# All 128 rows for the small products of a hybrid encoder block, and three norm factors spread by transpositions

## The chip, the cores and the metric

The kernel runs on one core of one Trainium2 chip. The metric is the device time of one execution in microseconds (us); the time given for a kernel is the median of its runs. The chip's engines work side by side, each on its own queue: TensorE (PE; its weight loads are shown apart, as PEld), VectorE (DVE), ScalarE (ACT), GpSimd (POOL), and SyncE (SP), which issues most of the DMA transfers.

## The reference

One layer of a bidirectional encoder on 512 tokens of 1024 channels, with 16 learned meta tokens put in front (528 positions), all in float32:

```
u      = rms_norm(h)
proj   = u @ w_in                                   # split into the parts below
z      = centred_shift(p_rwkv)                      # r, k, v, wd, ad, gd
w_log  = -softplus(-(w0 + tanh(wd) @ w2)) - 0.5     # per direction, rank 64
decay  = exp(-exp(w_log))
a      = sigmoid(a0 + ad @ a2)                      # per direction, rank 64
g      = sigmoid(gd) @ g2                           # rank 160
kk     = (k * k_k) / norm of each head              # the key norm
S_t    = S_{t-1} * decay + (S_{t-1} @ -kk) (kk*a)^T + v k^T ;  y_t = S_t r   # two directions
y_a    = (group_norm(y) + bonus) * g
y_b    = grouped-query attention: q, k rms-normed per head, axial rotary
h      = h + (sigmoid(gA)*(y_a @ wba) + sigmoid(gB)*(y_b @ wbb)) @ w_out
h      = h + square(relu(rms_norm(h) @ w_ff1)) @ w_ff2
out    = rms_norm(h)[:, 16:]
```

The products `tanh(wd) @ w2`, `ad @ a2` and `sigmoid(gd) @ g2` are the low-rank stage. There are 8 heads of 64 channels in the scan, and 8 query heads over 2 key heads in the attention.

## The kernel before, in words

**Precision.** A float32 product is made from products of a rounded type (`F32R`): each operand is split into a high part (a rounded copy, made by ScalarE) and a low part (the difference, made by VectorE or GpSimd), and three of the four part products are summed in PSUM (`mm3`, lines 130 to 134). Weights come in blocks of 128x1024, are split by `wblock` (lines 120 to 128: a DMA, ScalarE for `whi`, VectorE for `wlo`) and have two buffers each. A product whose operands stay plain float32 takes two TensorE instructions, each with its own weight load.

**The first norm.** The input projections of the low-rank part run on x without the norm (`project_steps`, lines 191 and 192). The norm's factor of each token stands in a column per 128 tokens. It is copied over 128 columns (`rx`) and multiplied with the identity matrix, which spreads it along the tokens: line 269 for the four blocks of tokens, line 272 for the meta tokens. `RT` holds the result; `scaled` multiplies by it (lines 275 to 284).

**The low-rank stage.** `stacked` (lines 329 to 337) keeps for each direction d one tile with 128 rows: the high part of the compressed activations in one half, the low part in the other. `constants` (lines 305 to 327) prepares the matrices. For `w2` and `a2` it makes `hh[d]`, the high part copied into both halves (line 316, ScalarE), and `lo`, whose two halves are the low parts of the two directions (line 317, GpSimd). So a product over 128 rows with `hh[d]` gives high times high plus low times high, and a product over the 64 rows of one half with `lo` adds high times low.

- Decay, lines 498 to 516: for each direction and block of 128 tokens, line 506 (128 rows) and line 507 (64 rows) into one PSUM bank, then `w0` is added (line 509, VectorE), the sigmoid (line 510, ScalarE) goes into a tile with the tag `sg` (three buffers), and its split into `sgh` and `sgl` follows (lines 513 and 514). Direction 0 has a fifth block, the 16 meta tokens; its `sg` tile is not split but used as it is.
- Heads, lines 517 to 541: for each direction and each of four pairs of heads, a product with a triangle matrix sums the decays (line 532). For direction 0 the meta tokens have products of their own, in plain float32: line 525 (16 rows) and line 526 (64 rows). Lines 537 (128 rows) and 538 (64 rows) give the rate `a`. Results go to DRAM, from where the scan's preparation reads them.
- Gate, lines 542 to 549: `mm3` on the first 128 ranks, and line 546 on the other 32, whose high and low parts are stacked in 96 rows (`gs`, `sst`).

The PSUM tag `rw` has two banks, which all these products share. Projections of the scan's r, k and v (lines 191 and 192) and the queries (lines 132 to 134) are interleaved with them.

**The scan.** `prepare`, `invert` and `chain` run as generators, with the gate projections fed in between. In `key_norm` (lines 577 to 607) the factors of the keys' norms are spread as in the first norm: line 603 for the tokens, line 598 for the 16 meta tokens, from a tile `rxm` of 16 rows. Most products of the scan use 64 rows or 64 columns.

**The attention.** `attend` (lines 1036 to 1086) runs per head and per half of the queries. The product of the probabilities with the values is line 1076 and line 1077 for four blocks of 128 keys, and line 1078 for the 16 meta keys: `vm` and `pms` have 48 rows, with the high parts in rows 0 to 15, the low parts in rows 32 to 47 and zeros between.

**The feed-forward part.** Its norm factor is spread at line 1223 in the same way as at line 269, and used after the first products of that part.

**Order.** The instructions are traced in program order; a planner then orders each engine's queue by priority with modelled times, gives out the buffers of each tag as they come free, and inserts the waits. `issue_after` keeps some products behind a given one. Each engine's queue is then fixed.

Of the kernel before, what the change touches and what calls it, by code (L numbers as in the profile page):

```python
# [7 lines left out]
F32R = mybir.dt.float32r  # L8
AF = mybir.ActivationFunctionType
ALU = mybir.AluOpType  # L10
# [4 lines left out]
P = 128  # L15
DM = 1024
NM = 16
SEQ = 512
L = NM + SEQ
# [30 lines left out]
def block_kernel(tc, A, out, dbg=None):  # L50
    nc = tc.nc
    v, s, g, pe, sy = nc.vector, nc.scalar, nc.gpsimd, nc.tensor, nc.sync
# [32 lines left out]
    with root:  # L85
# [18 lines left out]

        der = T(cp, [P, 36])
        DC_C0, DC_KKH, DC_KAH, DC_KAB, DC_A0H, DC_RKH = 0, 16, 20, 24, 28, 0
        tmpc = T(cp, [P, 16])
        rkh = T(cp, [P, 4])
        def dcol(c):
            return der[:, c:c + 1]  # L110
# [40 lines left out]
        with ph1:  # L151
# [74 lines left out]
            with ExitStack() as es:  # L226
# [14 lines left out]
                w13 = wblock(A["wrk"][13])  # L241
                sy.dma_start(cst, A["cst"])
                ps12 = whole(project_steps(first, raw))
                g.tensor_tensor(tmpc, par[:, PC_MU0:PC_MU0 + 16], par[:, PC_MU1:PC_MU1 + 16], op=ALU.add)
                g.tensor_scalar(der[:, 0:16], tmpc, -1.0, 1.0, op0=ALU.mult, op1=ALU.add)
                g.tensor_scalar(der[:, 16:20], par[:, PC_KK:PC_KK + 4], 0.5, None, op0=ALU.mult)
# [19 lines left out]
                whole(project_steps(A["wrk"][14], raw, ps14))  # L266
                ps = T(chp, [P, 512], tag="xu", bufs=1)
                for i in range(4):
                    pe.matmul(ps[:, i * P:(i + 1) * P], rx[:, i], ident, start=True, stop=True)
                s.copy(RT[:, NM:L], ps)  # L270
                ps = T(chp, [P, 512], tag="yp", bufs=1)
                pe.matmul(ps[:, 0:NM], rx[:, 4], ident[:, 0:NM], start=True, stop=True)
                s.copy(RT[:, 0:NM], ps[:, 0:NM])

                def scaled(ps):
# [29 lines left out]
                def constants():  # L305

                    c = {}
                    trr = T(wpy, [P, 2, P], F32R)
                    g.tensor_copy(trr, tri)
                    c["tri"] = trr  # L310
                    for n, t in (("w2", w2), ("a2", a2)):
                        hh = [T(wpy, [P, 512], F32R) for _ in range(2)]
                        lo = T(wpy, [P, 512], F32R)
                        for d in range(2):
                            for o in (d, 1 - d):
                                s.copy(hh[d][HF[o]], t[HF[d]])
                            g.tensor_tensor(lo[HF[d]], t[HF[d]], hh[d][HF[d]], op=ALU.subtract)
                        c[n] = hh, lo
                    gh, gl = T(wpy, [P, 512], F32R), T(wpy, [P, 512], F32R)
                    s.copy(gh, gw0)  # L320
                    g.tensor_tensor(gl, gw0, gh, op=ALU.subtract)
                    gs = T(wpy, [96, 512], F32R)
                    for x in (0, 2):
                        s.copy(gs[32 * x:32 * x + 32], gw1)
                    v.tensor_tensor(gs[32:64], gw1, gs[0:32], op=ALU.subtract)
                    c["gw"] = gh, gl, gs
                    return c

# [156 lines left out]
                sh, sl = T(wpz, [P, SEQ], F32R), T(wpz, [P, SEQ], F32R)  # L485
                s.copy(sh, sgd0)
                v.tensor_tensor(sl, sgd0, sh, op=ALU.subtract)
                sst = T(wpz, [96, SEQ], F32R)
                for x in range(2):
                    s.copy(sst[32 * x:32 * x + 32], sgd1)  # L490
                v.tensor_tensor(sst[64:96], sgd1, sst[0:32], op=ALU.subtract)
                keys_values(tk_, qkg, identr)
                xes.close()
                wpy = pool(es, "wdy")
# [3 lines left out]
                with tc.issue_after(started):  # L498
                    sgs = {}
                    for d in range(2):  # L500
                        for i in range(4 if d else 5):
                            n = P if i < 4 else NM
                            c = 64 + i * P if i < 4 else 48
                            ps = bank()
                            hh, lo = con["w2"]
                            pe.matmul(ps[0:n, :], wds[d][:, c - 48:c - 48 + n], hh[d], start=True, stop=False)
                            pe.matmul(ps[0:n, :], wds[d][HF[d], c - 48:c - 48 + n], lo[HF[d]], start=False, stop=True)
                            sg = T(wpy, [P, 512], tag="sg", bufs=3)
                            v.tensor_tensor(sg[0:n, :], ps[0:n, :], w0b[0:n, d, :], op=ALU.add)
                            s.activation(sg[0:n], sg[0:n], AF.Sigmoid)  # L510
                            if i < 4:
                                sgh, sgl = T(wpy, [P, 512], F32R, tag="sgh", bufs=8), T(wpy, [P, 512], F32R, tag="sgl", bufs=8)
                                s.copy(sgh, sg)
                                g.tensor_tensor(sgl, sg, sgh, op=ALU.subtract)
                                sg = sgh, sgl
                            sgs[d, i] = sg
                    for d in range(2):
                        for hp in range(NHP):
                            hc = slice(hp * P, (hp + 1) * P)
                            ab = dcol(DC_A0H + d * 4 + hp)  # L520
                            x0 = 0 if d == 0 else NM
                            lo_ = T(wpy, [P, 2, L], tag="lo", bufs=3)
                            if d == 0:
                                pm = bank()
                                pe.matmul(pm[:, 0:NM], sgs[0, 4][0:NM, hc], tri[0:NM, 0, 0:NM], start=True, stop=True)
                                pe.matmul(pm[:, 16:32], a2[0:64, hc], adz[0:64, 48:64], start=True, stop=True)
                                v.tensor_copy(lo_[:, 0, 0:NM], pm[:, 0:NM])
                                s.activation(lo_[:, 1, 0:NM], pm[:, 16:32], AF.Tanh, scale=0.5, bias=ab)
                            ps = bank()
                            for i in range(4):  # L530
                                for x in range(2):
                                    pe.matmul(ps[:, i * P:(i + 1) * P], sgs[d, i][x][:, hc], con["tri"][:, d, :], start=x == 0, stop=x == 1)
                            v.tensor_copy(lo_[:, 0, NM:L], ps)
                            sy.dma_start(cs_d[hp, d][:, x0:L], lo_[:, 0, x0:L])
                            ps = bank()
                            hh, lo = con["a2"]
                            pe.matmul(ps, hh[d][:, hc], ads[d][:, NM:L], start=True, stop=False)
                            pe.matmul(ps, lo[HF[d], hc], ads[d][HF[d], NM:L], start=False, stop=True)
                            s.activation(lo_[:, 1, NM:L], ps, AF.Tanh, scale=0.5, bias=ab)
                            sy.dma_start(th_d[hp, d][:, x0:L], lo_[:, 1, x0:L])  # L540
                    for hp in range(NHP):
                        hc = slice(hp * P, (hp + 1) * P)
                        ps = bank()
                        gh, gl, gs = con["gw"]
                        mm3(ps, gh[:, hc], gl[:, hc], sh, sl, True, False)
                        pe.matmul(ps, gs[:, hc], sst, start=False, stop=True)
                        gg = T(wpy, [P, SEQ], tag="gg", bufs=2)
                        v.tensor_copy(gg, ps)
                        sy.dma_start(g_d[hp], gg)
# [2 lines left out]

            gtp = pool(ph1a, "gt1", side="right")
            rp = pool(ph1, "rw")
            def load_rkv(hp):
                zs = []
                for x in range(3):
# [19 lines left out]
            def key_norm(hp, zk):  # L577
# [11 lines left out]
                power_mhalf(rn[0:NM, 8:10], rn[0:NM, 8:10])  # L589
                yield  # L590
                rx = G()
                rxm = T(rp, [NM, P], tag="rxm", bufs=1)
                v.tensor_copy(rx[:, 0:512].rearrange("p (a b) -> p a b", b=64), rn[:, 0:8].unsqueeze(2).broadcast_to([P, 8, 64]))
                v.tensor_copy(rxm.rearrange("p (a b) -> p a b", b=64), rn[0:NM, 8:10].unsqueeze(2).broadcast_to([NM, 2, 64]))
                kkh = G("k")
                g.memset(kkh[:, 0:48], 0.0)
                ps = bank()
                pe.matmul(ps[:, 0:NM], rxm, ident[0:NM, 0:NM], start=True, stop=True)
                v.scalar_tensor_tensor(kkh[:, 48:64], zk[:, 48:64], dcol(DC_KKH + hp), ps[:, 0:NM],
                                       op0=ALU.mult, op1=ALU.mult)  # L600
                ps = bank()
# [417 lines left out]
            kll = T(ap_, [P, 2, L], F32R)  # L1019
            vv = T(ap_, [P, 4, 2, P], F32R)  # L1020

            vm = T(ap_, [48, 2, P], F32R)
            pms = [T(ap_, [48, 256], F32R) for _ in range(2)]
            for part, t in ((0, khh), (1, kll)):
                sy.dma_start(t.bitcast(F32), kt_d[part])
            for i in range(4):
                sy.dma_start(vv[:, i].bitcast(F32), vv_d[i])
            lpp = pool(aes, "aloop", side="right")
            zz = T(lpp, [P, 256], tag="yo", bufs=2)[0:48]
            g.memset(zz, 0.0)  # L1030
            for pm in (vm.rearrange("p a b -> p (a b)"), *pms):
                v.tensor_copy(pm, zz)
# [100 lines left out]
        with ExitStack() as es:  # L1133
# [86 lines left out]
            v.tensor_copy(rx, ss[:, 12:16].unsqueeze(2).broadcast_to([P, 4, P]))  # L1220
            ps = fbank("t")
            for i in range(4):
                pe.matmul(ps[:, i * P:(i + 1) * P], rx[:, i, :], ident, start=True, stop=True)
            s.copy(RS, ps)
        dump("h1", h1)

# [150 lines left out]
```

## Time and profile before

| | |
|---|---|
| median of 3 runs | 1050.72 us (1048.79 to 1052.95) |
| the profiled execution | 1051.4 us, of it 1049.6 in the profile's span |
| mean granted TensorE clock in it | 0.968 |
| instructions | 17962 |

The span is what the profile covers; the rest of the execution's time lies around it. The engine lines of a page give busy time, share of the span and number of instructions. A row of a timeline gives start and length in us, engine, line, operation, tiles, rows*columns of the array, the size of what is streamed, and the count; in brackets stands the idle time before it. TensorE's lengths overlap, so the step from one start to the next is what a product costs while nothing else is waited for. A group row gives busy time and mean ns of one, then the idle time before and what ended it. Line numbers are those of the kernel before.

### The profile page before, as it was taken

What the parts mean: (1) busy time and instruction counts of PE and PEld (TensorE: products, weight loads), DVE (VectorE), ACT (ScalarE), POOL (GpSimd) and SP (SyncE); (2) the same over time, 40 slices, a digit from 0 to 9 for tenths busy, and PEclk for the clock granted to TensorE, in tenths of its full rate; (3) what the DMA queues carried; (4) which work ended last, traced back from release to release, by engine and by line L of the source; (5) the groups of instructions that cost most, each with busy time, mean ns of one, the idle gap of its engine ahead of it and who ended that gap; (6) DMA issues with size and microseconds to landing.
All of it is one profiled execution on the core that took longest, in us unless ns stands there. A gap on an engine that the chain in (4) does not pass through costs nothing.

```text
span 1049.6 us, 17962 instructions
## 1 busy us (share of the span) xinstructions
PE 994.9 (95%) x7208; PEld 816.1 (78%) x7208; DVE 592.2 (56%) x1084; ACT 434.4 (41%) x802; POOL 185.9 (18%) x373
## 2 busy tenths in 40 slices
PE   7799989989999899989989999999999999999996
PEld 7778978877767676767777788888888888888885
DVE  4967647756663737396977566455555552123123
ACT  6676434424322524275788533343332232113112
POOL 1266411411411132112311123000000000001001
PEclk9999999999989899886999999999999999999999
DMA  9233662232222211510010284222233332322322
GB/s 348 70 113 86 197 239 71 72 117 100 80 93 92 82 62 62 174 42 11 12 32 21 82 269 132 83 86 95 98 101 101 101 109 92 101 92 89 101 96 85
DMA packets 45508, 107.25 MB, mean 102 GB/s; under 512 B 5264, under 2 KB 12736, under 8 KB 45424
## 3 DMA queue, kind: packets, MB, share of 16 engines
q1 hardware_dynamic: 44848, 105.05, 30.7%
q8 instruction: 57, 0.93, 0.4%
q10 hardware_dynamic: 576, 1.05, 0.3%
q14 instruction: 27, 0.22, 0.1%
HBM read 87.54 MB, written 18.54 MB: 101 GB/s over the span
## 4 chain that ended last, share of the span: by engine, by line
PE 81%; DVE 10%; ACT 4%; issue 2%; DMA 2%; POOL 0%; SPq 0%; ACTq 0%; DVEq 0%; POOLq 0%
PE f L134 8%; PE f L133 8%; PE f L132 8%; PE t L132 6%; PE t L133 6%; PE t L134 6%; PE mm L132 5%; PE mm L133 4%; PE mm L134 4%; PE mm L191 4%; PE mm L192 3%; PE rw L705 2%; PE rw L813 2%; PE yp L869 1%; PE xu L847 1%
## 5 line engine op out<-in xcount | busy, mean ns | idle before, releaser
L126 ACT CAST whi<-wraw 128x1024 fp32r<-128x1024 f32 x118 | 123.7, 1050 | 321.9 <-PE f L134 76.8
L127 DVE TENSOR_TENSOR wlo<-wraw,whi 128x1024 fp32r<-128x1024 f32 x118 | 148.6, 1260 | 183.8 <-ACT whi L126 183.4
L191 PE MATMUL mm<-t,whi 128*128 128x264 f32 x240 | 70.0, 309 | 7.6 <-ACT t L239 7.5
L132 PE MATMUL f<-t,whi 128*128 128x512 f32 x184 | 72.0, 392 | 0.0
L133 PE MATMUL f<-t,whi 128*128 128x512 f32 x184 | 71.7, 390 | 0.0
L134 PE MATMUL f<-t,wlo 128*128 128x512 f32 x184 | 70.9, 390 | 0.0
L192 PE MATMUL mm<-t,whi 128*128 128x264 f32 x240 | 67.7, 299 | 0.0
L133 PE MATMUL t<-wlo,t 128*128 128x512 f32 x160 | 63.4, 396 | 0.0
L133 PE MATMUL f<-wlo,t 128*128 128x512 f32 x160 | 63.3, 396 | 0.0
L134 PE MATMUL f<-whi,t 128*128 128x512 f32 x160 | 63.3, 396 | 0.0
L134 PE MATMUL t<-whi,t 128*128 128x512 f32 x160 | 63.3, 395 | 0.0
L132 PE MATMUL mm<-t,whi 128*128 128x512 f32 x128 | 58.1, 454 | 0.0
L191 PEld LDWEIGHTS mm<-t,whi 128*128 128x128 f32 x240 | 47.9, 199 | 10.8 <-ACT t L239 7.5
L132 PE MATMUL t<-whi,t 128*128 128x512 f32 x160 | 54.7, 397 | 0.0
L132 PE MATMUL f<-whi,t 128*128 128x512 f32 x160 | 53.9, 395 | 0.0
L132 PE MATMUL t<-t,whi 128*128 128x512 f32 x136 | 53.2, 393 | 0.2 <-ACT whi L126 0.2
L134 PE MATMUL t<-t,wlo 128*128 128x512 f32 x136 | 53.0, 391 | 0.0
L133 PE MATMUL t<-t,whi 128*128 128x512 f32 x136 | 52.6, 389 | 0.0
L133 PE MATMUL mm<-t,whi 128*128 128x512 f32 x128 | 52.2, 408 | 0.0
L134 PE MATMUL mm<-t,wlo 128*128 128x512 f32 x128 | 52.0, 406 | 0.0
L1266 POOL TENSOR_TENSOR t<-t,t 128x512 f32<-128x512 f32 x4 | 5.1, 1302 | 261.0 <-DVE t L1263 261.0
L192 PEld LDWEIGHTS mm<-t,whi 128*128 128x128 f32 x240 | 47.9, 200 | 1.5 <-issue 1.4
(338 smaller groups left out, 2372.6 us busy)
## 6 DMA issues: line engine op xcount, KB each, us to landing
wraw<-in_w SPq DMA_DIRECT2D x32, 512.0 KB, 3.4
wraw<-in_w2f SPq DMA_DIRECT2D x32, 512.0 KB, 3.4
wraw<-in_wrk SPq DMA_DIRECT2D x16, 512.0 KB, 3.9
wraw<-in_wg SPq DMA_DIRECT2D x16, 512.0 KB, 3.7
t<-gt SPq DMA_DIRECT2D x16, 256.0 KB, 2.0
gt<-t SPq DMA_DIRECT2D x16, 256.0 KB, 3.3
wraw<-in_wo SPq DMA_DIRECT2D x8, 512.0 KB, 3.4
g<-t SPq DMA_DIRECT2D x12, 256.0 KB, 3.4
```

The lines of the kernel that those rows point to most:

```text
L126: s.copy(hi, raw)
L127: v.tensor_tensor(lo, raw, hi, op=ALU.subtract)
L132: pe.matmul(o, ah, bh, start=first, stop=False)
L133: pe.matmul(o, ah, bl, start=False, stop=False)
L134: pe.matmul(o, al, bh, start=False, stop=last)
L191: pe.matmul(pa, wt[:, w], ut[:, k, 0:264], start=first, stop=last)
L192: pe.matmul(pb, wt[:, w], ut[:, k, 264:528], start=first, stop=last)
L705: pe.matmul(ps[:, c - a, :, :], bkh(h, c), xr[HR[h], h:h + 2, c, :], start=True, stop=True)
L813: pe.matmul(ps[HR[h], cc], hs[HR[h], cc], cur[HR[h], cc], start=True, stop=True)
L847: pe.matmul(X[HR[h], j], ps[d]["xr"][:, 2 * h, c, :], svu[:, c, h, :], start=True, stop=True)
L869: pe.matmul(yp[HR[h], j], svu[:, c, h, :], ps[d]["rl"][:, h, c, :], start=False, stop=last and j == 1)
L1266: (v if half else g).tensor_tensor(o[:, i, cols], h1[:, i, cols], fg[:, cols], op=ALU.mult)
```

## The change

Products with fewer than 128 rows get operands of 128 rows. `lo` becomes two tiles, each with one direction's low part in both halves, and lines 507 and 538 use them whole, which adds the small product low times low; the copies into the second half are ScalarE's. To make room, `sg` has two buffers instead of three. The meta tokens' `sg` tile is cleared before it is written, and line 525 uses all its rows. Line 526 becomes two products of the split constants. `gs` and `sst` get a fourth group of 32 rows. `rxm` is one tile of 128 rows, cleared once. `vm` and `pms` have 128 rows, of which the unused ones are zero. Lines 269, 272 and 1223 use `transpose` in place of a product with the identity. A small tile, `tmpc`, moves to another pool.

```diff
                 ps = T(chp, [P, 512], tag="xu", bufs=1)
                 for i in range(4):
-                    pe.matmul(ps[:, i * P:(i + 1) * P], rx[:, i], ident, start=True, stop=True)
+                    pe.transpose(ps[:, i * P:(i + 1) * P], rx[:, i], ident)
...
-                pe.matmul(ps[:, 0:NM], rx[:, 4], ident[:, 0:NM], start=True, stop=True)
+                pe.transpose(ps[:, 0:P], rx[:, 4], ident)
...
                         hh = [T(wpy, [P, 512], F32R) for _ in range(2)]
-                        lo = T(wpy, [P, 512], F32R)
+                        lo = [T(wpy, [P, 512], F32R) for _ in range(2)]
                         for d in range(2):
                             for o in (d, 1 - d):
                                 s.copy(hh[d][HF[o]], t[HF[d]])
-                            g.tensor_tensor(lo[HF[d]], t[HF[d]], hh[d][HF[d]], op=ALU.subtract)
+                            g.tensor_tensor(lo[d][HF[d]], t[HF[d]], hh[d][HF[d]], op=ALU.subtract)
+                            s.copy(lo[d][HF[1 - d]], lo[d][HF[d]])
...
-                    gs = T(wpy, [96, 512], F32R)
+                    gs = T(wpy, [P, 512], F32R)
                     for x in (0, 2):
                         s.copy(gs[32 * x:32 * x + 32], gw1)
-                    v.tensor_tensor(gs[32:64], gw1, gs[0:32], op=ALU.subtract)
+                        v.tensor_tensor(gs[32 * x + 32:32 * x + 64], gw1, gs[0:32], op=ALU.subtract)
...
-                sst = T(wpz, [96, SEQ], F32R)
+                sst = T(wpz, [P, SEQ], F32R)
                 for x in range(2):
                     s.copy(sst[32 * x:32 * x + 32], sgd1)
-                v.tensor_tensor(sst[64:96], sgd1, sst[0:32], op=ALU.subtract)
+                    v.tensor_tensor(sst[64 + 32 * x:96 + 32 * x], sgd1, sst[0:32], op=ALU.subtract)
...
-                            pe.matmul(ps[0:n, :], wds[d][HF[d], c - 48:c - 48 + n], lo[HF[d]], start=False, stop=True)
-                            sg = T(wpy, [P, 512], tag="sg", bufs=3)
+                            pe.matmul(ps[0:n, :], wds[d][:, c - 48:c - 48 + n], lo[d], start=False, stop=True)
+                            sg = T(wpy, [P, 512], tag="sg", bufs=2)
+                            if i == 4:
+                                g.memset(sg, 0.0)
...
-                                pe.matmul(pm[:, 0:NM], sgs[0, 4][0:NM, hc], tri[0:NM, 0, 0:NM], start=True, stop=True)
-                                pe.matmul(pm[:, 16:32], a2[0:64, hc], adz[0:64, 48:64], start=True, stop=True)
+                                pe.matmul(pm[:, 0:NM], sgs[0, 4][:, hc], tri[:, 0, 0:NM], start=True, stop=True)
+                                for x in range(2):
+                                    pe.matmul(pm[:, 16:32], con["a2"][x][0][:, hc], ads[0][:, 0:NM], start=x == 0, stop=x == 1)
...
-                            pe.matmul(ps, lo[HF[d], hc], ads[d][HF[d], NM:L], start=False, stop=True)
+                            pe.matmul(ps, lo[d][:, hc], ads[d][:, NM:L], start=False, stop=True)
...
             rp = pool(ph1, "rw")
+            rxm = T(rp, [P, P])
+            g.memset(rxm, 0.0)
...
-                rxm = T(rp, [NM, P], tag="rxm", bufs=1)
-                v.tensor_copy(rxm.rearrange("p (a b) -> p a b", b=64), rn[0:NM, 8:10].unsqueeze(2).broadcast_to([NM, 2, 64]))
+                v.tensor_copy(rxm[0:NM].rearrange("p (a b) -> p a b", b=64), rn[0:NM, 8:10].unsqueeze(2).broadcast_to([NM, 2, 64]))
...
-                pe.matmul(ps[:, 0:NM], rxm, ident[0:NM, 0:NM], start=True, stop=True)
+                pe.matmul(ps[:, 0:NM], rxm, ident[:, 0:NM], start=True, stop=True)
...
-            vm = T(ap_, [48, 2, P], F32R)
-            pms = [T(ap_, [48, 256], F32R) for _ in range(2)]
+            vm = T(ap_, [P, 2, P], F32R)
+            pms = [T(ap_, [P, 256], F32R) for _ in range(2)]
...
-            zz = T(lpp, [P, 256], tag="yo", bufs=2)[0:48]
+            zz = T(lpp, [P, 256], tag="yo", bufs=2)
...
-                pe.matmul(ps[:, i * P:(i + 1) * P], rx[:, i, :], ident, start=True, stop=True)
+                pe.transpose(ps[:, i * P:(i + 1) * P], rx[:, i, :], ident)
```

More of the change, by code (lines that the diff above doesn't have):

```diff
@@ L106, in block_kernel @@
         DC_C0, DC_KKH, DC_KAH, DC_KAB, DC_A0H, DC_RKH = 0, 16, 20, 24, 28, 0
-        tmpc = T(cp, [P, 16])
         rkh = T(cp, [P, 4])
@@ L243, in block_kernel @@
                 ps12 = whole(project_steps(first, raw))
+                tmpc = T(xp, [P, 16])
                 g.tensor_tensor(tmpc, par[:, PC_MU0:PC_MU0 + 16], par[:, PC_MU1:PC_MU1 + 16], op=ALU.add)
```

## The prediction

> **What bounds the kernel now.** I read the page first: engine shares and the chain that ended last.
>
> ```profile
> PE 994.9 (95%) x7208; PEld 816.1 (78%) x7208; DVE 592.2 (56%) x1084; ACT 434.4 (41%) x802; POOL 185.9 (18%) x373
> ...
> PE 81%; DVE 10%; ACT 4%; issue 2%; DMA 2%; POOL 0%; SPq 0%; ACTq 0%; DVEq 0%; POOLq 0%
> ```
>
> The reader is to see that TensorE carries 81% of the chain; VectorE, with 10%, is a distant second. That is an average, so the second view was the table of stretches, cut where the changed products stand: the end of the low-rank stage's preparation and its decay products (50 to 98 us), the heads of that stage (101 to 145), and a stretch of the attention.
>
> ```profile
> 50.00:76.00 26.00, 26.00 (x152) 21.74 (x152) 17.59 (x46) 19.81 (x43) 16.52 (x27) 1.00 0.34 102
> 76.00:98.00 22.00, 22.00 (x120) 16.39 (x119) 14.63 (x20) 14.78 (x28) 11.68 (x11) 1.00 0.37 98
> 101.00:145.00 44.00, 44.00 (x327) 39.38 (x326) 26.44 (x43) 21.45 (x36) 14.69 (x18) 1.00 0.61 194
> 480.00:500.00 20.00, 18.84 (x155) 14.62 (x154) 14.57 (x34) 10.63 (x26) 6.17 (x20) 0.74 0.05 14
> ```
>
> The columns are the length, then the busy time of PE, PEld, DVE, ACT and POOL with instruction counts, the granted clock, the DMA share and GB/s. From 50 to 98 and from 101 to 145 us PE is busy without a hole at clock 1.00, and no other engine is busy for more than 76% (ACT, 19.81 of 26). PE's own time is what these stages cost. The attention differs: PE, DVE and ACT hand work to one another, and the granted clock there was 0.74.
>
> Third, PE's timeline around the products to be changed. A busy share says nothing about how tightly products follow each other; start to start does.
>
> ```profile
> 79.11 0.39 PE L133 MATMUL mm<-wlo,t 128*128 128x512 f32 x1
> 79.35 0.39 PE L134 MATMUL mm<-whi,t 128*128 128x512 f32 x1
> ...
> 106.66 0.29 PE L191 MATMUL mm<-t,whi 128*128 128x264 f32 x1
> 106.79 0.40 PE L537 MATMUL rw<-t,t 128*128 128x512 f32 x1
> 107.11 0.49 PE L538 MATMUL rw<-t,t 64*128 64x512 f32 x1
> 107.53 0.39 PE L192 MATMUL mm<-t,whi 128*128 128x264 f32 x1
> 107.76 0.28 PE L191 MATMUL mm<-t,whi 128*128 128x264 f32 x1
> ...
> 145.26 0.50 PE L132 MATMUL rw<-t,t 128*128 128x512 f32 x1
> ...
> 146.06 0.40 PE L546 MATMUL rw<-t,t 96*128 96x512 f32 x1
> 146.29 0.39 PE L132 MATMUL rw<-t,t 128*128 128x512 f32 x1
> ```
>
> A product of 128 rows and 512 columns gives way to the next after 0.24 us (79.11 to 79.35), one of 264 columns after 0.13 (106.66 to 106.79). Around line 538, which uses 64 rows, the steps are 0.32, 0.42 and 0.23 us. Line 546 with 96 rows steps by 0.23 (146.06 to 146.29): it costs nothing extra, so its widening to 128 rows is taken at zero. The weight loads of the same place show where the time goes.
>
> ```profile
> 106.66 0.19 PEld L537 LDWEIGHTS rw<-t,t 128*128 128x128 f32 x1
> 107.11 0.18 PEld L538 LDWEIGHTS rw<-t,t 64*128 64x128 f32 x1 [0.26 <-issue]
> ```
>
> The load for line 537 (128 rows) starts at 106.66 with the product before its own, and is hidden. The load for line 538 waits until 107.11: a change of the number of rows, in either direction, puts a load in the open.
>
> **The change, part by part.** The counts come from the groups by shape.
>
> ```profile
> L1078 PE MATMUL tp<-t,t 48*128 48x256 f32 x16 | 6.5, 407 | 0.0
> L507 PE MATMUL rw<-t,t 64*128 64x512 f32 x8 | 4.0, 496 | 0.0
> L538 PE MATMUL rw<-t,t 64*128 64x512 f32 x8 | 4.0, 495 | 0.0
> L598 PE MATMUL rw<-t,rxm 16*128 16x16 f32 x8 | 2.0, 324 | 0.2 <-DVE rxm L594 0.2
> L526 PE MATMUL rw<-t,t 64*128 64x16 f32 x8 | 1.6, 270 | 0.0
> ```
>
> *Lines 507 and 538.* From 106.79 to 107.76 three steps take 0.97 us; at full rows they would take 0.24 + 0.24 + 0.13 = 0.61. One excursion to 64 rows costs 0.36 us. Sixteen of them: 5.8 us. A ninth product of line 507 with 16 output columns (the meta tokens) is counted at zero.
>
> *Lines 525 and 526,* once per head of the first direction:
>
> ```profile
> 109.83 0.28 PE L191 MATMUL mm<-t,wlo 128*128 128x264 f32 x1
> 110.04 0.39 PE L525 MATMUL rw<-t,sg 16*128 16x16 f32 x2
> 110.36 0.39 PE L526 MATMUL rw<-t,t 64*128 64x16 f32 x2
> 110.68 0.40 PE L192 MATMUL mm<-t,wlo 128*128 128x264 f32 x1
> 110.91 0.28 PE L191 MATMUL mm<-t,whi 128*128 128x264 f32 x1
> ```
>
> 1.08 us from 109.83 to 110.91. The changed form also has four instructions: two passes of the float32 product, and two products of the split constant in one pass each. The nearest row for a small one-pass step is the transposition of line 1063 below (0.44 us for four, 0.11 each). So 0.13 + 4 x 0.11 + 0.13 = 0.70, and 0.38 less for each of four heads: 1.5 us.
>
> *Line 1078, attention,* sixteen times, after either kind of neighbour:
>
> ```profile
> 534.18 0.28 PE L1077 MATMUL tp<-ptl,t 128*128 128x256 f32 x1
> 534.39 0.38 PE L1078 MATMUL tp<-t,t 48*128 48x256 f32 x1
> 534.71 0.39 PE L1053 MATMUL sc<-t,qs 128*128 128x264 f32 x1
> 534.94 0.28 PE L1054 MATMUL sc<-t,qs 128*128 128x264 f32 x1
> ...
> 552.29 0.38 PE L1078 MATMUL tp<-t,t 48*128 48x256 f32 x1
> 552.61 0.39 PE L869 MATMUL yp<-g,g 128*64 128x64 f32 x5
> ```
>
> Before a full product: 0.76 us for three steps, against 3 x 0.13: 0.37 saved. Before a product of the scan (552.61, 64 output columns) the next product differs in shape anyway. Of the 0.08 extra at entry (0.21 less 0.13) and the 0.19 at exit (0.32 less 0.13), the entry's 0.08 stays, at the new place: 0.19 saved. I take the middle, 0.28; sixteen give 4.5 us of PE time. Here PE is not alone on the path (18.84 busy of 20, DVE 14.57 in the row of 480), so it is worth between 0 and 4.5. I take 3.0, nearer to the upper end, since PE is the busiest engine by 4 us in 20.
>
> *Line 598, key norm,* eight instructions in four heads. They stand among products of the scan with 64 rows or columns, so most switches stay. Between 0 and 8 x 0.11 = 0.9 us; I take 0.3.
>
> *The spreads by transposition* (lines 269, 272, 1223):
>
> ```profile
> 22.90 0.91 PE xu L269 x8
> ...
> 540.33 0.44 PE tp L1063 x4
> ```
>
> Both are rows of the chain. Four float32 products with the identity take eight instructions and 0.91 us; four transpositions of the same size take 0.44. Line 1223 has the same form and count as line 269: 2 x 0.47 = 0.9 us, and 0.1 for line 272. Line 269 lies on the chain while VectorE waits for the spread factor. Line 1223's PE time lies in a stage in which PE never stops.
>
> *What is added.* ScalarE: four copies of 64x512 for the second halves of the low parts. VectorE: two subtractions over 32 rows. POOL: one clear of a 128x512 tile and one of 128x128. VectorE and POOL have 8 and 9 us free in the row of 50 us, which hides theirs. ScalarE's:
>
> ```profile
> 66.75 5.09 ACT L316 CAST t<-t 64x512 fp32r<-64x512 f32 x8
> ```
>
> 0.64 us each, 2.5 together. Queued behind them on ScalarE is the split of the last block of query weights; PE waits for it if that cover is gone. Between 0 and 2.5 us; ScalarE is idle for 6 of 26 us there, so I take 0.5. Removing the tag from the key-norm tile and the move of one small tile to another pool cost nothing.
>
> *The sum.* Low rank 5.8 + 1.5 = 7.3 us, of which 0.7 is taken off because the end of that stage is a tail of evictions and DMAs that PE doesn't set: 6.6. Attention 3.0, key norm 0.3, spreads 1.0, additions -0.5: 10.4 us. The profiled execution took 1051.4 us (span 1049.6 and 1.8 around it), 0.7 above the median of 1050.7. So 1041.0 on its scale, 1040.3 on the median's: I say 1040.
>
> **One rule against it.** The Trainium skill ("TensorE: Matmul & The Clock Gate", Part 3, on what overlaps) says that in the traces behind it weight loads ran beside products in flight only where the row groups differ. By it a product on all rows hides no load, and widening 64 rows to 128 gains nothing. This case's trace disagrees: the load of line 537, all rows, ran from 106.66 beside line 191's product, all rows, and it is the 64-row load that waited. The sum by that rule would be the spreads' 1.0 alone.
>
> **The rivals.** *A: the attention and key norm hide their share.* Every output there waits for ScalarE, VectorE and back, and a shorter PE step lets DVE end last. For it: DVE's 14.57 of 20 us. Against: PE's 18.84. Then 6.6 + 1.0 - 0.5 = 7.1 remains: 1043.6.
>
> *B: other interleaving.* The planner lays out the queues from modelled times, so changed steps reorder the scan and the attention. Where that opens holes, PE may also run slower: the row of 480 us has the clock at 0.74, up to 0.26 x 20 = 5 us lost in one such stretch. One stretch more: 1045.5. Nothing in the profile says which way it falls.
>
> *C: the gap isn't made by the rows,* but by, say, the operands' place. Then the change doesn't do what it says; spreads less additions leave 1050.2. Against it: lines 537 and 538 stream the same tile into the same bank, and 96 rows (line 546) step like 128.
>
> *D, slower: two buffers instead of three for the sigmoid tiles (tag "sg").* The meta tokens' tile stays held until line 525 of the fourth head has read it, so the four tiles of the second direction pass through one buffer, one after the other.
>
> ```profile
> 101.63 0.68 DVE L509 TENSOR_TENSOR sg<-rw,t 128x512 f32<-128x512 f32 x1
> ...
> L514 POOL TENSOR_TENSOR sgl<-sg,sgh 128x512 fp32r<-128x512 f32 x8 | 11.0, 1385 | 9.2 <-ACT sgh L513 9.2
> ...
> 131.49 0.84 PE rw L532 x8
> ```
>
> Per tile 0.68 on DVE, two ScalarE steps (by line 316's 0.64) and 1.39 on POOL: 3.4 us, four 13.4. Queued behind an add that waits are DVE's weight splits, and PE waits for those. Now the last add is at 101.63, 30 us ahead of its reader at 131.49. Nothing is lost while the train starts before 131.5 - 13.4 = 118; each us later costs up to one. If it starts only when the reader stands, 13.4 are lost against 3.0 + 0.3 + 1.0 gained elsewhere: 1050.7 + 9.1 = 1060. It ends over 0.5% slower from a start at about 128 on.
>
> **How the numbers follow.** A measurement of this kernel can tell about 0.5%, 5.3 us, from no change: the bounds are 1045.5 and 1056. Forecast (1040) 0.56; A (1043.6) 0.18; B (1045.5, half on each side of the bound) 0.16; C 0.05; D 0.05. Faster 0.56 + 0.18 + 0.08 = 0.82; same 0.08 + 0.05 = 0.13; slower 0.05. The range: all bounds at their best give 7.3 + 4.5 + 0.9 + 1.0 = 13.7, so 1037, and B can fall to the good side by some 3 us: 1034. Upward it takes in A with additions at 2.5 (1045.6) and most of B: 1047.
>
> **What would show it.** Right: lines 507, 538 and 1078 step by 0.23 to 0.24 and 0.12 to 0.13 with their loads hidden; lines 269 and 1223 have four instructions in 0.45 us; the first gate product (line 132 of the rw bank, now at 145.26) starts 6 to 8 us earlier. Wrong: the steps stay at 0.3 and more (C); the low-rank stage ends as late as before, with adds of line 509 waiting for a buffer (D); or the gain is there at 150 us and gone by 600 (A, B). The prediction falls if the scan and the attention together are longer than before.

## The result, and the profile after

The changed kernel took 1042.22 us (median), the kernel before 1051.84 in the same comparison: the ratio is 0.9895 with a 95% interval of 0.9856 to 0.9933. A second comparison on another occasion gave 1040.16 against 1053.52, ratio 0.9879 (0.9852 to 0.9906). One of the changed kernel's first four executions took 1941 us, with its products nearly twice as long (line 190: 543 ns against 305) for a reason that is open, and is left out of the ratio; since it was the profiled one, all lines "after" below are from the second comparison, whose profiled execution took 1041.5 us. Line numbers of the changed kernel differ by a few from those of before.

The page of the changed kernel, the lines that answer to those of before:

```profile
span 1039.6 us, 17948 instructions
...
PE 981.6 (94%) x7199; PEld 810.9 (78%) x7199; DVE 595.7 (57%) x1086; ACT 436.9 (42%) x806; POOL 187.9 (18%) x375
...
PE 78%; DVE 12%; ACT 4%; DMA 2%; issue 2%; POOL 1%; SPq 0%; ACTq 0%; DVEq 0%; POOLq 0%
```

PE's busy time fell by 13.3 us (994.9 to 981.6), the span by 10.0. The same four stretches of time:

```profile
50.00:76.00 26.00, 25.83 (x149) 21.64 (x148) 19.61 (x47) 20.11 (x42) 16.39 (x27) 1.00 0.32 103
76.00:98.00 22.00, 22.00 (x148) 19.86 (x147) 15.94 (x23) 16.68 (x32) 12.24 (x13) 1.00 0.41 121
101.00:145.00 44.00, 42.25 (x303) 38.21 (x302) 29.92 (x43) 21.78 (x37) 16.51 (x24) 0.92 0.65 212
480.00:500.00 20.00, 18.27 (x209) 14.40 (x207) 19.25 (x52) 13.59 (x32) 11.72 (x34) 1.00 0.04 14
```

From 76 to 98 us PE gets through 148 products instead of 120 in the same time. But from 101 to 145 it has holes now (42.25 of 44), and the granted clock there is 0.92 where it was 1.00. PE's timeline around the products of the rate, of the meta tokens and of the meta keys, and the weight loads of the first:

```profile
122.95 0.39 PE L541 MATMUL rw<-t,t 128*128 128x512 f32 x1
123.18 0.40 PE L542 MATMUL rw<-t,t 128*128 128x512 f32 x1
123.41 0.28 PE L191 MATMUL mm<-t,whi 128*128 128x264 f32 x1
123.53 0.28 PE L190 MATMUL mm<-t,whi 128*128 128x264 f32 x1
...
124.14 0.29 PE L528 MATMUL rw<-t,sg 128*128 128x16 f32 x2
124.28 0.37 PE L530 MATMUL rw<-t,t 128*128 128x16 f32 x2
124.50 0.37 PE L191 MATMUL mm<-t,whi 128*128 128x264 f32 x1
...
562.33 0.28 PE L1082 MATMUL tp<-ptl,t 128*128 128x256 f32 x1
562.45 0.28 PE L1083 MATMUL tp<-t,t 128*128 128x256 f32 x1
562.57 0.28 PE L1058 MATMUL sc<-t,qs 128*128 128x264 f32 x1
562.69 0.28 PE L1059 MATMUL sc<-t,qs 128*128 128x264 f32 x1
```

```profile
122.95 0.19 PEld L542 LDWEIGHTS rw<-t,t 128*128 128x128 f32 x1
123.18 0.19 PEld L191 LDWEIGHTS mm<-t,whi 128*128 128x128 f32 x1
```

At the rate (lines 541 and 542) the steps are 0.23, 0.23 and 0.12 us where they were 0.32, 0.42 and 0.23; at the meta keys (line 1083) they are 0.12 each where they were 0.21, 0.32 and 0.23. The load of line 542 starts with the product before its own. So the mechanism is the forecast one. The Trainium skill ("TensorEngine Tiling (Array Packing)", Key Properties) says that a change of the tiling mode drains TensorE. These rows and those of before fit that, though they show a load that waits and not the drain itself.

Where the span's 10 us came from is read from landmarks of the trace (starts in us; "half" is the time between 150 and 600 us in which the trace's record of the granted clock shows one half):

| kernel | last sigmoid add | first triangle product | first gate product | first key norm | first scores | last meta keys | spread, line 1223 | span | half |
|---|---|---|---|---|---|---|---|---|---|
| before | 101.6 | 104.9 | 145.3 | 152.2 | 443.4 | 590.7 | 691.2 | 1049.6 | 58.0 |
| after | 112.6 | 110.9 | 144.4 | 150.1 | 441.0 | 580.5 | 681.2 | 1039.6 | 47.8 |
| low-rank stage alone | 112.3 | 110.5 | 144.3 | 150.2 | 442.1 | 585.7 | 686.4 | 1044.8 | 37.5 |
| the same, second profile | 112.8 | 111.1 | 144.6 | 150.5 | 449.9 | 595.8 | 696.6 | 1055.0 | 68.3 |
| attention alone | 101.5 | 104.8 | 145.1 | 151.5 | 446.8 | 590.3 | 690.5 | 1048.9 | 64.9 |
| attention, 96 rows | 101.5 | 104.8 | 145.2 | 151.8 | 441.1 | 584.6 | 685.3 | 1043.6 | 47.8 |
| spreads alone | 101.1 | 104.4 | 144.8 | 151.3 | 444.1 | 588.5 | 689.3 | 1047.7 | 47.8 |
| the same, second profile | 101.0 | 104.3 | 144.6 | 151.0 | 455.2 | 606.1 | 706.9 | 1065.3 | 99.0 |
| after, attention as before | 112.9 | 111.0 | 145.2 | 151.8 | 441.0 | 588.3 | 688.8 | 1047.2 | 52.4 |
| after, three sigmoid buffers | 98.9 | 101.8 | 138.6 | 146.7 | 440.0 | 579.2 | 690.7 | 1049.1 | 56.4 |
| low-rank stage, three buffers | 100.4 | 103.3 | 140.0 | 146.1 | 438.8 | 577.4 | 688.7 | 1047.1 | 44.4 |
| before, two sigmoid buffers | 114.8 | 114.6 | 148.1 | 154.5 | 445.2 | 587.4 | 688.1 | 1046.5 | 58.4 |
| after, more spreads by transposition | 112.3 | 110.6 | 144.3 | 150.7 | 455.4 | 600.8 | 701.7 | 1060.1 | 75.1 |

Of the 10.0 us, 2.1 are there at the first key norm, 2.4 at the first scores and 10.2 at the last product with the meta keys: most of it appears not in the low-rank stage but in the stretch of the attention.

### The profile page after: what moved, and what is told of

Read it like the earlier page. It is cut to its first block, busy times and chain, and to the rows that moved or that the text cites. A ratio compares the mean times of both kernels' runs of the same rounds, so it can differ in the third digit from the quotient of the medians.

```text
span 1939.3 us, 17948 instructions
## 1 busy us (share of the span) xinstructions
PE 1913.9 (99%) x7199; PEld 1390.4 (72%) x7199; DVE 590.4 (30%) x1086; ACT 441.8 (23%) x806; POOL 174.8 (9%) x375
## 4 chain that ended last, share of the span: by engine, by line
PE 98%; ACT 1%; DVE 0%; DMA 0%; issue 0%; POOL 0%; POOLq 0%; SPq 0%
PE f L131 8%; PE f L132 8%; PE f L133 8%; PE t L132 7%; PE t L133 7%; PE t L131 7%; PE mm L190 6%; PE mm L191 6%; PE mm L131 5%; PE mm L132 5%; PE mm L133 5%; PE rw L710 3%; PE rw L818 3%; PE tp L1068 2%; PE yp L874 1%; PE xu L852 1%
## 5 line engine op out<-in xcount | busy, mean ns | idle before, releaser
L126 DVE TENSOR_TENSOR wlo<-wraw,whi 128x1024 fp32r<-128x1024 f32 x118 | 145.2, 1231 | 443.0 <-ACT whi L125 442.9
L190 PE MATMUL mm<-t,whi 128*128 128x264 f32 x240 | 130.1, 543 | 7.1 <-ACT t L238 7.0
L191 PE MATMUL mm<-t,whi 128*128 128x264 f32 x240 | 128.6, 537 | 0.0
L131 PE MATMUL f<-t,whi 128*128 128x512 f32 x184 | 124.6, 678 | 0.0
L132 PE MATMUL f<-t,whi 128*128 128x512 f32 x184 | 124.6, 677 | 0.0
L133 PE MATMUL f<-t,wlo 128*128 128x512 f32 x184 | 122.9, 672 | 0.0
L133 PE MATMUL t<-whi,t 128*128 128x512 f32 x160 | 108.9, 681 | 0.0
L132 PE MATMUL f<-wlo,t 128*128 128x512 f32 x160 | 108.4, 677 | 0.0
L133 PE MATMUL f<-whi,t 128*128 128x512 f32 x160 | 106.0, 663 | 0.0
L190 PEld LDWEIGHTS mm<-t,whi 128*128 128x128 f32 x240 | 93.8, 391 | 12.5 <-ACT t L238 7.0
L191 PEld LDWEIGHTS mm<-t,whi 128*128 128x128 f32 x240 | 97.7, 407 | 2.6 <-issue 2.5
L131 PE MATMUL f<-whi,t 128*128 128x512 f32 x160 | 96.7, 683 | 0.0
L131 PE MATMUL t<-whi,t 128*128 128x512 f32 x160 | 96.2, 668 | 0.0
L131 PE MATMUL t<-t,whi 128*128 128x512 f32 x136 | 92.3, 681 | 0.0
L132 PE MATMUL t<-t,whi 128*128 128x512 f32 x136 | 91.7, 675 | 0.0
L132 PE MATMUL mm<-t,whi 128*128 128x512 f32 x128 | 91.3, 713 | 0.0
L131 PE MATMUL mm<-t,whi 128*128 128x512 f32 x128 | 89.5, 699 | 0.0
L132 PEld LDWEIGHTS f<-t,whi 128*128 128x128 f32 x184 | 55.0, 299 | 31.3 <-issue 29.2
```

The lines of the kernel that those rows point to most:

```text
L126: v.tensor_tensor(lo, raw, hi, op=ALU.subtract)
L131: pe.matmul(o, ah, bh, start=first, stop=False)
L132: pe.matmul(o, ah, bl, start=False, stop=False)
L133: pe.matmul(o, al, bh, start=False, stop=last)
L190: pe.matmul(pa, wt[:, w], ut[:, k, 0:264], start=first, stop=last)
L191: pe.matmul(pb, wt[:, w], ut[:, k, 264:528], start=first, stop=last)
```

## The experiments

Theory R is the prediction's: a change of the number of rows puts a weight load in the open. C is its rival that the rows don't matter, A that the attention hides the gain, B that the order of the queues and the clock decide, D that two sigmoid buffers cost time. The later expectations write D' for D as it concerns the low-rank stage's gain, and T for its rival that the tail of that stage sets its end in any case.

**The changed kernel, again.**

> The changed kernel as it is, for a profile at the same granted clock as that of before. Theory R (a change of the number of rows puts a weight load in the open, and full rows hide it): the steps after the products of the decay, of the rate and of the meta keys are 0.23 to 0.24 us for 512 columns and 0.12 to 0.13 for 256; the gate's first product starts 6 to 8 us earlier than 145.3; 1040 to 1043 us. Theory C (the rows don't make the gap): those steps stay at 0.3 to 0.4 us.

Measured: 1040.16 us, ratio 0.9879 (0.9852 to 0.9906). The steps are as R has them; C is out. The gate's first product moved by 0.9 us, not by 6 to 8.

**The low-rank stage alone:** the hunks on `lo`, `sg`, lines 525, 526, `gs` and `sst`.

```diff
-                            pe.matmul(ps, lo[HF[d], hc], ads[d][HF[d], NM:L], start=False, stop=True)
+                            pe.matmul(ps, lo[d][:, hc], ads[d][:, NM:L], start=False, stop=True)
...
-                            sg = T(wpy, [P, 512], tag="sg", bufs=3)
+                            sg = T(wpy, [P, 512], tag="sg", bufs=2)
```

> Only the low-rank stage has 128 rows (lines 507, 538, 525, 526, 546), with the added copies and two sigmoid buffers; attention, key norm and spreads as before. Theory R: 7.3 us of PE time less, 0.7 hidden in the tail and 0.5 of additions: -6.1 us, 1044 to 1046. Theory C: +0.5. Theory D (two sigmoid buffers stall VectorE and PE): the adds of the second direction move to 118 us or later, and the time is above that of before by up to 13.

Measured: 1056.38 us, ratio 1.0032 (1.0008 to 1.0056), runs from 1046.6 to 1061.1. R's 1044 to 1046 us is missed. D's total, above that of before, came, but not its sign: the last add is at 112.3 us and not at 118 or later, and the profile has the gate 1.0 us earlier. This total is taken up again with the scatter below.

**The attention alone.**

```diff
-            vm = T(ap_, [48, 2, P], F32R)
-            pms = [T(ap_, [48, 256], F32R) for _ in range(2)]
+            vm = T(ap_, [P, 2, P], F32R)
+            pms = [T(ap_, [P, 256], F32R) for _ in range(2)]
```

> Only the product of the meta keys in the attention has 128 rows. Theory R with PE at the end of most waits: -3.0 us. Rival A (VectorE and ScalarE set the end there): 0 to -1. Theory C: 0. Rival B (the planner's order): between -5 and +5 with changed order in the scan.

Measured: 1048.11 us, ratio 0.9950 (0.9927 to 0.9972). The total fell by more than A allows, and R's -3.0 lies at the edge of the interval. From the first scores to the last meta keys the stage takes 143.5 us instead of 147.2, but that alone doesn't tell R from B: by the table it takes 143.6 in the low-rank stage alone and 144.5 in the spreads alone, whose attention is as before.

**The spreads alone.**

```diff
-                    pe.matmul(ps[:, i * P:(i + 1) * P], rx[:, i], ident, start=True, stop=True)
+                    pe.transpose(ps[:, i * P:(i + 1) * P], rx[:, i], ident)
```

> Only the three spreads by transposition. Eight instructions become four at two places and two become one: the prediction's term is -1.0 us. If ScalarE's copies and VectorE's scaling hide the first one: -0.5.

Measured: 1060.19 us, ratio 1.0042 (1.0007 to 1.0076), runs from 1049.5 to 1067.3. The chain has the first spread at 0.67 us for four (0.91 for eight before), and the first key norm is 0.9 us earlier. The total came out above that of before, where -1.0 was forecast; with runs that scatter by 18 us it is read with the clock, below.

**Three sigmoid buffers in the changed kernel.** The changed kernel's two buffers moved the adds. These are the meta tokens' row (16 rows) of the kernel before, and VectorE's rows of the changed kernel from 93 us on:

```profile
89.06 0.68 DVE L509 TENSOR_TENSOR sg<-rw,t 16x512 f32<-16x512 f32 x1 [0.98 <-PE rw L507]
```

```profile
93.65 0.68 DVE L512 TENSOR_TENSOR sg<-rw,t 128x512 f32<-128x512 f32 x1
96.22 0.67 DVE L512 TENSOR_TENSOR sg<-rw,t 16x512 f32<-16x512 f32 x1
98.01 0.67 DVE L512 TENSOR_TENSOR sg<-rw,t 128x512 f32<-128x512 f32 x1
104.78 0.68 DVE L512 TENSOR_TENSOR sg<-rw,t 128x512 f32<-128x512 f32 x1
112.61 0.68 DVE L512 TENSOR_TENSOR sg<-rw,t 128x512 f32<-128x512 f32 x1
```

The room for a third buffer comes from letting the tile `adz` share the buffers of another tag, so two things change.

```diff
-                adz = T(wpz, [P, 576])
+                adz = T(wpz, [P, 576], tag="gz", bufs=2)
...
-                            sg = T(wpy, [P, 512], tag="sg", bufs=2)
+                            sg = T(wpy, [P, 512], tag="sg", bufs=3)
```

> The changed kernel with three sigmoid buffers again; the room comes from letting the tile of the shifted rate activations use the two buffers of tag gz. Theory D' (the ring of two, with the meta tile pinned in one, ate the low-rank stage's gain: last add at 112.6 us instead of 101.6, clock halved at 137.6): last add back at 100 to 104 us, first triangle product at about 104 instead of 110.9, the gate's first product at 139 to 142 instead of 145.8, total 4 to 6 us under the changed kernel. Rival T (the tail of banks, evictions and DMAs sets the stage's end in any case): the adds move back, the gate's product stays at 144 to 146, total as the changed kernel's within 1.5 us.

Measured: 1050.54 us, ratio to before 0.9983 (0.9963 to 1.0003): 10 us slower than the changed kernel, where 4 to 6 us less were expected. (The 145.8 us of this expectation and the 146.1 of the next are the gate's narrow product, line 550 or 546, and not its first.) In the stage itself D' holds:

```profile
85.89 0.68 DVE L512 TENSOR_TENSOR sg<-rw,t 16x512 f32<-16x512 f32 x1 [0.20 <-PE rw L508]
...
98.93 0.68 DVE L512 TENSOR_TENSOR sg<-rw,t 128x512 f32<-128x512 f32 x1
```

The meta tokens' add is 10.3 us earlier, the last 13.7, and the gate begins at 138.6 instead of 144.4. By the first scores, 5.8 us of lead have become 1.0, and at the end they are a loss. The chain of waits of this kernel and that of the changed one, where the scan's last norm is made:

```profile
595.10 0.38 PE yp L874 x8
...
607.26 0.79 PE rw L916 x8
...
614.33 0.91 PE rw L925 x8
```

```profile
587.55 0.79 PE rw L916 x8
...
596.88 0.89 PE rw L925 x8
```

The attention ends at almost the same time in both (579.2 and 580.5), but the scan's last steps come 17 to 20 us later, with products of the attention's branch between them. The scan's branch needs their result, and by then nothing is left to cover it. The stretches from 610 us, first with three buffers, then the changed kernel:

```profile
610.00:620.00 10.00, 5.66 (x29) 4.71 (x28) 2.27 (x4) 1.43 (x2) 1.30 (x2) 0.97 0.67 220
620.00:630.00 10.00, 9.55 (x35) 7.05 (x35) 7.51 (x9) 3.25 (x4) 3.68 (x3) 0.86 0.44 140
```

```profile
610.00:620.00 10.00, 10.00 (x46) 8.29 (x45) 7.92 (x9) 3.91 (x5) 6.24 (x4) 1.00 0.88 321
620.00:630.00 10.00, 10.00 (x46) 8.20 (x45) 9.69 (x10) 4.09 (x6) 5.73 (x5) 1.00 0.57 176
```

PE stands for over 4 us and runs part of the next ten at half clock; from the last meta keys to the feed-forward spread it takes 111.5 us instead of 100.7. This order is the planner's: in PE's queue, 132 products into the tile `f` (the attention's branch) stand ahead of the scan's last spread, line 925, here and in the low-rank stage alone with three buffers, and 61 in every other kernel of the table. That is rival B, at a place that the edit doesn't touch.

**Two sigmoid buffers in the kernel before.**

> The kernel before with two sigmoid buffers and nothing else. Theory D': last add at 110 us or later, the gate's first product 2 to 6 us later than 146.1, total +2 to +6 us. Rival T, or the ring being hidden as the prediction had it: total within 1 us of before.

Measured: 1051.50 us, ratio 0.9995 (0.9968 to 1.0023). Both halves are true: the last add moves to 114.8 and the gate by 2.8 us, and the total doesn't show it. In the profile the attention, which this edit doesn't touch, makes up for it: 142.2 us from the first scores to the last meta keys instead of 147.2.

**The low-rank stage alone, with three buffers** (the edits of the two kernels above together).

> Only the low-rank stage with 128 rows, and three sigmoid buffers. Theory D': the prediction's -6.1 us is now there: gate's first product at 139 to 142 us, total -4 to -7 against before. Rival T: as with two buffers, about 0 to +3.

Measured: 1051.59 us, ratio 0.9982 (0.9959 to 1.0005). The gate begins 5.3 us earlier than before (145.3 to 140.0) and the key norm 6.1 (152.2 to 146.1), close to the forecast 6.6; then the same wait at the end of the scan (111.3 us to the spread) takes it, and the expected 4 to 7 us in the total are not there.

**96 rows in the attention.**

```diff
-            vm = T(ap_, [48, 2, P], F32R)
+            vm = T(ap_, [96, 2, P], F32R)
```

> The kernel before with the meta keys' product on 96 rows (rows 48 to 95 zero) instead of 48. If a load is hidden as soon as more than 64 rows are used, as line 546 with 96 rows suggests: steps of 0.12 to 0.13 us before and after it where the neighbours have 128 rows, as with 128 rows in the run of the attention alone. If only equal numbers of rows hide it: 0.21 and 0.31 as with 48.

Measured once: 1045.43 us. PE's timeline of this kernel:

```profile
566.37 0.28 PE L1077 MATMUL tp<-ptl,t 128*128 128x256 f32 x1
566.48 0.28 PE L1078 MATMUL tp<-t,t 96*128 96x256 f32 x1
566.60 0.28 PE L1053 MATMUL sc<-t,qs 128*128 128x264 f32 x1
566.72 0.28 PE L1054 MATMUL sc<-t,qs 128*128 128x264 f32 x1
```

Steps of 0.11 and 0.12: 96 rows are as good as 128. The stage takes 143.5 us, as with 128. So the prediction's sentence that a change of the number of rows puts a load in the open is too wide: 48 and 64 rows between products of 128 do, 96 don't.

**The changed kernel with the attention as before.**

> The changed kernel with the meta keys' product on 48 rows again; everything else as changed. If that product is the larger part of the gain (the attention alone gave 0.995, some 5 us): 4 to 6 us above the changed kernel, 1044 to 1047. By the prediction's term: 3 us above. If the gain lies in how the queues happen to be ordered: anything up to the time of before, 1052, with the low-rank stage's profile up to 150 us unchanged.

Measured: 1048.82 us, ratio to before 0.9960 (0.9938 to 0.9982), by the two ratios some 8.5 us above the changed kernel and so above both expected values, 3 and 4 to 6. Up to the first scores the two profiles agree (441.0); then the stage takes 147.2 us against 139.5. So here the sixteen products bring 7.7 us in the stage, twice the 3.7 of the attention alone; a part of both is the clock's.

**More spreads by transposition:** those of the key norm and of the scan's last norm too.

```diff
-                    pe.matmul(ps[:, i * P:(i + 1) * P], rx[:, i * P:(i + 1) * P], ident, start=True, stop=True)
+                    pe.transpose(ps[:, i * P:(i + 1) * P], rx[:, i * P:(i + 1) * P], ident)
```

> The changed kernel with the spreads of the key norm and of the scan's last norm (four each) as transpositions too. Each takes four instructions instead of eight: 8 x 0.45 = 3.6 us of PE time less, in the scan where half of it hides: -1.5 to -2 us against the changed kernel, 1038 to 1040. If the order of the queues decides: between 1035 and 1052.

Measured: 1061.23 us, ratio to before 1.0080 (1.0058 to 1.0102): 21 us slower than the changed kernel for less work on PE. From key norm to first scores it takes 304.7 us against 290.9, and 75.1 us between 150 and 600 lie at half clock against 47.8. No expectation had that: even the one for the order of the queues ended at 1052. At the price of half clock found below, the 27.3 us more make some 9 of the 20.5 us by which the two spans differ; what makes the rest was not found.

**The scatter of the runs:** second profiles of two kernels.

> The spreads alone once more, for a second profile: its runs lay between 1049.5 and 1067 us, and the profiled one was the shortest. If the granted clock makes that spread: a longer run has more time at half clock in the scan and the attention (over 48 us between 150 and 600, against 47.7 in the first profile), with the same queue orders. If something else does (DMA landing times): the same time at half clock, and a longer wait for a transfer at one place.

> The low-rank stage alone once more, for a second profile: its runs lay between 1046.6 and 1061 us, and the profiled one was the shortest. As for the spreads alone: more time at half clock than the first profile's 37.5 us between 150 and 600 if the clock makes the spread; one longer wait for a transfer if not.

Measured: 1067.09 and 1056.77 us. The stretches of the spreads alone, first and second profile of the same program:

```profile
0.00:150.00 150.00, 135.90 (x883) 117.66 (x883) 101.13 (x163) 93.40 (x160) 55.32 (x88) 0.99 0.53 175
150.00:450.00 300.00, 280.11 (x2882) 227.91 (x2884) 179.44 (x405) 109.50 (x227) 72.13 (x203) 0.94 0.28 93
450.00:600.00 150.00, 137.14 (x1516) 109.55 (x1513) 116.89 (x278) 106.83 (x252) 32.78 (x64) 0.97 0.11 32
600.00:1040.00 440.00, 438.38 (x1925) 357.40 (x1924) 191.63 (x234) 122.34 (x159) 23.09 (x16) 1.00 0.33 105
```

```profile
0.00:150.00 150.00, 136.07 (x883) 118.01 (x883) 101.13 (x163) 93.50 (x160) 55.51 (x88) 0.99 0.53 175
150.00:450.00 300.00, 280.33 (x2770) 226.31 (x2770) 173.28 (x387) 104.66 (x214) 67.43 (x195) 0.90 0.26 85
450.00:600.00 150.00, 141.42 (x1519) 115.61 (x1520) 114.32 (x279) 104.10 (x248) 33.02 (x70) 0.86 0.12 36
600.00:1040.00 440.00, 438.40 (x1959) 356.75 (x1958) 193.54 (x239) 125.50 (x168) 24.54 (x17) 1.00 0.34 109
```

Up to 150 us the two are alike; in the scan and the attention the clock column falls from 0.94 and 0.97 to 0.90 and 0.86, and fewer products are done by 450 us. PE's queue has the same order in both. The half-clock time rose from 47.8 to 99.0 us and the span by 17.6: 0.34 us for each. For the low-rank stage alone, 37.5 to 68.3 and 10.2 us: 0.33. The clock makes the scatter.

The record, which has the mean granted clock of every run, says the same: in the 81 runs of the kernel before it lies between 0.954 and 0.971, and a straight line through these runs falls by 7.6 us per 0.01 and leaves a scatter of 1 us around it. So kernels can be compared at one clock. Reading each kernel's own line at 0.965 gives these estimates, good to about 1 us, and to 2 us in the two rows marked *, whose runs all lie to one side of 0.965:

| kernel | median clock | us at 0.965 |
|---|---|---|
| before | 0.967 | 1052.9 |
| before, two sigmoid buffers | 0.961 | 1048.6 |
| low-rank stage alone (two buffers) | 0.957 | 1051.3 |
| low-rank stage, three buffers | 0.966 | 1053.3 |
| attention alone | 0.968 | 1049.3 |
| spreads alone | 0.953 | 1054.3 |
| after, attention as before | 0.968 | 1049.7 |
| after * | 0.970 | 1044.1 |
| after, three sigmoid buffers | 0.966 | 1051.0 |
| after, more spreads by transposition * | 0.955 | 1057.9 |

From before to after there is a path with one edit at a time: two sigmoid buffers -4.3, full rows in the low-rank stage +2.7, spreads and key norm -1.6, full rows in the attention -5.6. On another path the terms would differ, as the attention's does (-3.6 alone), and where an edit itself changed the clock, that is left out of its term.

## Why the prediction came out as it did

**The total:** 1040 was forecast, 1042.2 and 1040.2 were measured. Two of its terms were wrong by about as much, in opposite directions, and by the estimates at one clock the buffer that was priced as a risk brought more than the low-rank stage's rows.

**The price of a step** held: an excursion from 512-column products cost 0.39 us (0.97 to 0.58) where 0.36 was forecast, the meta keys' 0.40 (0.76 to 0.36) where it was 0.37, and PE's busy time fell by 13.3 us where the unhidden sum of all bounds was 13.7. The Trainium skill's rule ("TensorE: Matmul & The Clock Gate", Part 3) that only loads to other row groups are hidden, and with it rival C, would have left the steps as they were.

**Low rank, 6.6 us: wrong as applied.** The gate began 0.9 us earlier and the key norm 2.1. The step that failed is rival D's sentence "Nothing is lost while the train starts before 118". I watched the train of the second direction and not the meta tokens' tile, which now waits for a buffer too: its add moved from 89.1 to 96.2 us, the first triangle product from 104.9 to 110.9, and the heads then came too late: PE has 1.75 us of holes from 101 to 145 and 10.2 us at half clock from 137.6 on (that the late heads brought the half clock is not shown). With three buffers the gate began 6.7 us earlier than before: at the gate, the term was right for the kernel with three. In the total it was not right with either: at one clock, full rows in this stage brought no gain (2.7 us slower with two buffers, 0.4 with three). With three, what the stage gave is lost at the end of the scan; where it goes with two was not found. The prediction counted a gain at 150 us as a gain at the end.

**Attention, 3.0 us: too small here.** Alone it measured 3.7 us in the stage. Between the first scores and the last meta keys the record of the clock shows one half for 24.2 us before, 20.7 with the attention alone and 17.4 in the changed kernel; at 0.34 us each (0.24 to 0.27 by the same two pairs of profiles in this stage alone), the 3.5 us less make 0.9 to 1.2 of the 3.7. In the whole change the stage gained 7.7, with 6.8 us less at half clock (1.7 to 2.3). That leaves 2.5 to 2.8 and 5.4 to 6.0. Why it is worth more in the whole change is not settled: the stage also fell to 138.6 us in the low-rank kernel with three buffers and to 142.2 in the kernel before with two, whose attention is unchanged, so order has a hand in it.

**Key norm and spreads, 1.3 us:** line 1228's four transpositions take the forecast 0.44 us on the chain, but line 269's take 0.67, so the spread itself is 0.24 us shorter where 0.47 was forecast. The first key norm is 0.9 us earlier with the spreads alone; the others are too small to be seen. In the total at one clock, the spreads alone are 1.4 us slower, and spreads and key norm together 1.6 faster on the path above.

**B was priced at 5 us and put at 0.16.** It was too small on both counts: kernels that differ little lie from 1040 to 1061, and at one clock still from 1044 to 1058; the parts' ratios (0.9950, 1.0032, 1.0042) don't add up to the whole's 0.9879, and five variants with less work on PE than before (the low-rank stage alone, the spreads alone, the low-rank stage with three buffers, the changed kernel with three, and the one with more spreads) were not measurably faster than it. In all three pairs here the kernel with two sigmoid buffers is faster at one clock than the one with three (by 4.3, 2.0 and some 7 us), which nothing in the prediction foresaw. The forecast's sign rested on a right mechanism; that the total landed where it did was luck in the order as well. The changed kernel's runs stay within 1038 to 1043 us, while those of before go from 1048 to 1061, since their clock stays within 0.968 to 0.973; why it does is open.

No kernel tried was faster than the changed one.

## What to carry to other kernels

In a dense stream on TensorE, products with 48 or 64 rows between full ones cost some 0.4 us more in steps here; zeros up to 96 or 128 rows removed that, and the start-to-start steps show it where busy time can't. Look at what the wider operands displace: here one buffer less in a ring undid the gain of the stage that it served, and changed the order so that the whole came out shorter all the same. And follow a gain of a few us to the end of the kernel by landmarks, in more than one profile, before it is believed, and compare runs at one granted clock: the planner's order and the clock moved as much as the edit did.

## What the runs showed of the hardware

The granted clock fell to one half in stretches of 3.4, 6.8, 10.2 us and more, most of them in the scan and the attention, where PE is busy for 93% of the time (280 of 300 us in the spreads alone, 150 to 450 us). The Trainium skill ("TensorE: Matmul & The Clock Gate", Part 1) gives half rate as the state beside full rate, and a free-running window of 3.413 us; the stretches' lengths agree. The same program took 17.6 us more than 1047.7 (1.7%) in another run, with 51.2 us more at half clock. What decides in which windows the clock falls was not tried.
